# Loading x in four DMAs of 32 KiB packets, one copy per engine and tile, and the first load ahead of the barrier, in a 2x nearest-neighbour upsample

## The chip, the cores and the metric

The kernel runs on one core of one Trainium2 chip. The metric is the device time in microseconds of one execution, lower is better. Each timed version ran several times, alternating with the kernel before on the same chip. The span of a profile, from its first to its last instruction, is 1.6 us or more shorter than the device time of the same run; I compare times with times and spans with spans.

## The reference

```python
batch, channels, h, w = (16, 64, 64, 64)            # float32, scale_factor 2
for i in range(new_h):
    for j in range(new_w):
        result[:, :, i, j] = x[:, :, i // scale_factor, j // scale_factor]
```

Nothing is computed. 16.8 MB are read and 67.1 MB written; each input element goes to four places.

## The kernel before

An input row has 64 floats, 256 bytes. A tile gives each of the 128 partitions 32 input rows (8 KiB), which become 32 KiB of output. Loads take two such tiles per DMA (the first two are loaded alone). VectorE and ScalarE expand half of the rows each, with four copies per tile, one for each of the 2x2 target places. All DMAs are issued by SyncE on one queue.

```python
K = 32; rows = P * K; J = 2
...                                   # cut: checks, the sizes of the pools; group = 8, u2 has 2 buffers
for ti in range(ti0, ti0 + group):
    xt = xpool.tile([P, J, K, W], fdt, name="xt")
    if ti == 0:
        for j in range(J):
            nc.sync.dma_start(out=xt[:, j, :, :],
                in_=xf[(ti * J + j) * rows : (ti * J + j + 1) * rows, :])
    else:
        src = xf[ti * J * rows : (ti + 1) * J * rows, :]
        src = src.rearrange("(j p k) w -> p j (k w)", j=J, p=P)     # 8 KiB runs
        nc.sync.dma_start(out=xt[:, :, :, :], in_=src)
...
for t in range(ti0 * J, (ti0 + group) * J):
    ...
    u2 = upool.tile([P, K, s, W, s], fdt, name="u2")
    for ei, (lo, hi) in enumerate(((0, k_dve), (k_dve, K))):
        for hd in range(s):
            for wd in range(s):
                dst = u2[:, lo:hi, hd, :, wd]
                ...                    # cut: VectorE's tensor_copy or ScalarE's copy
    nc.sync.dma_start(out=of[r0 : r0 + rows, :], in_=u2[:, :, :, :, :])
```

Of the kernel before, what the change touches and what calls it, by code (L numbers as in the profile page):

```python
# [1 line left out]

# [4 lines left out]


@with_exitstack  # L10
def kernel(
    ctx: ExitStack,
    tc: tile.TileContext,
    x: bass.AP,
    scale_factor: bass.AP,
    out: bass.AP,
):
    nc = tc.nc
    P = nc.NUM_PARTITIONS

    s = int(scale_factor) if not isinstance(scale_factor, bass.AP) else None
    assert s is not None and s >= 1

    B, C, H, W = x.shape
    R = B * C * H
    fdt = x.dtype
    esz = 4 if fdt == mybir.dt.float32 else mybir.dt.size(fdt)

    xf = x.rearrange("b c h w -> (b c h) w")
    of = out.rearrange("b c (h hd) w -> (b c h) (hd w)", hd=s)  # L30

    K = 32
    while K > 1 and R % (P * K) != 0:
        K //= 2
    assert R % (P * K) == 0, f"{R} input rows not tileable into {P} partitions"
    rows = P * K
    ntiles = R // rows
    J = 2
    while ntiles % J != 0:
        J //= 2  # L40
    n_in = ntiles // J

    u2_bytes = K * s * W * s * esz * 2
    xt_bytes = J * K * W * esz
    group = max(1, min(n_in, (200 * 1024 - u2_bytes) // xt_bytes))
    while n_in % group != 0:
        group -= 1

    k_dve = (K + 1) // 2

    with (
        tc.tile_pool(name="xin", bufs=group) as xpool,
        tc.tile_pool(name="uexp", bufs=2) as upool,
    ):
        for ti0 in range(0, n_in, group):
            xts = {}
            for ti in range(ti0, ti0 + group):
                xt = xpool.tile([P, J, K, W], fdt, name="xt")
                if ti == 0:
                    for j in range(J):  # L60
                        nc.sync.dma_start(
                            out=xt[:, j, :, :],
                            in_=xf[(ti * J + j) * rows : (ti * J + j + 1) * rows, :],
                        )
                else:
                    src = xf[ti * J * rows : (ti + 1) * J * rows, :]
                    if J > 1:
                        src = src.rearrange("(j p k) w -> p j (k w)", j=J, p=P)
                    nc.sync.dma_start(out=xt[:, :, :, :], in_=src)
                xts[ti] = xt  # L70

            for t in range(ti0 * J, (ti0 + group) * J):
                ti, j = divmod(t, J)
                r0 = t * rows
                xt = xts[ti]

                u2 = upool.tile([P, K, s, W, s], fdt, name="u2")
                for ei, (lo, hi) in enumerate(((0, k_dve), (k_dve, K))):
                    if lo >= hi:
                        continue  # L80
                    src_ap = xt[:, j, lo:hi, :]
                    for hd in range(s):
                        for wd in range(s):
                            dst = u2[:, lo:hi, hd, :, wd]
                            if ei == 0:
                                nc.vector.tensor_copy(out=dst, in_=src_ap)  # L86
                            else:
                                nc.scalar.copy(out=dst, in_=src_ap)  # L88

                nc.sync.dma_start(out=of[r0 : r0 + rows, :], in_=u2[:, :, :, :, :])  # L90


# [1 line left out]
_INS = ['x', 'scale_factor']  # L94
_OUTS = [((16, 64, 128, 128), 'float32')]
#: Inputs that are plain numbers.
_NUMBERS = {'scale_factor': 2}


# [26 lines left out]
```

## Time and profile before

| | before |
|---|---|
| time, median (before the prediction) | 200.79 us, 200.72 to 201.0, 3 runs |
| span of the profile | 199.2 us |
| first data packet | 1.74 us |
| packets in flight without a gap | 196.2 us |
| one 8 KiB load packet | 309 to 321 ns for 97% of them, mean 317 ns (2048 of them) |
| one 32 KiB store packet | 1213 ns (2048 of them) |

The packet rows are worked out from the start, length and size of each packet in the trace. Sixteen DMA engines share the packets, so n packets of t take n x t / 16.

Lines of the page of the kernel before: span, busy time, DMA by fortieths of the span, the two queues with packets, MB and share of 16 engines, the chain that ended last, and the two groups of copies (count | busy us, mean ns | idle us before, and what ended most of it).

```profile
span 199.2 us, 246 instructions
DVE 40.0 (20%) x64; ACT 68.0 (34%) x65; POOL 0.2 (0%) x4
DMA  6999999999999999999999999999999999999995
...
q1 hardware_dynamic: 4496, 83.89, 98.5%
q14 instruction: 3, 0.02, 0.0%
...
DMA out_dram<-u 67%; ACT u L88 18%; SPq L90 3%; DMA xt<-in_x_dram 2%; ACTq L121 1%; ACTq L88 0%
...
L88 ACT COPY u<-xt 128x1024 f32<-128x1024 f32 x64 | 66.7, 1136 | 114.6 <-DMA out_dram<-u 111.0
L86 DVE COPY u<-xt 128x1024 f32<-128x1024 f32 x64 | 40.0, 690 | 141.7 <-DMA out_dram<-u 136.1
```

The queue of transfers is never idle between the first and the last slice, and both compute engines mostly wait for a store to give back an output buffer. The 18% of ScalarE in the chain of waits do not mean that ScalarE costs anything: while it expands one buffer, the other buffer's store keeps the DMA engines busy. So the time is bytes over DMA rate, plus what is lost.

The timeline of SyncE's first two microseconds (start, length, what), and pieces of the chain of waits in order of time (start, length, what):

```profile
0.73 0.86 SPq L61 DMA_DIRECT2D xt<-in_x_dram  x2
1.64 0.43 SPq L69 DMA_DIRECT2D xt<-in_x_dram  x1
```

```profile
105.30 15.10 DMA out_dram<-u
...
124.69 15.14 DMA out_dram<-u
139.92 4.21 ACT u L88 x4
144.15 15.56 DMA out_dram<-u
159.81 4.18 ACT u L88 x4
164.01 15.02 DMA out_dram<-u
```

The first load is issued at 0.73 us, after a barrier.

Four stretches of the profile before (window, its length, busy times of VectorE, ScalarE, GpSimd, clock, DMA share, GB/s): loads, loads, the turnover from loads to stores, and stores.

```profile
4.00:20.00 16.00, 4.96 (x8) 8.25 (x8) 0.00 (x0) 1.00 1.01 426
20.00:36.00 16.00, 0.00 (x0) 0.00 (x0) 0.00 (x0) 1.00 1.01 421
36.00:48.00 12.00, 0.00 (x0) 0.00 (x0) 0.00 (x0) 1.00 1.02 433
48.00:185.00 137.00, 35.02 (x56) 58.46 (x56) 0.00 (x0) 1.00 1.01 434
```

Loads run at 421 to 426 GB/s, stores at 434. GB/s of a stretch count a packet where it starts, so with 32 KiB packets a short stretch is uncertain by 2 to 4%.

### The profile page before, as it was taken

To read this page: it belongs to the slowest core of one execution; us is meant where nothing else is said; L and a number is where in the kernel's file an instruction comes from. 1 tells how busy PE (TensorE), PEld (TensorE's weight loads), DVE (VectorE), ACT (ScalarE), POOL (GpSimd) and SP (SyncE) were. 2 spreads that over 40 slices of the span, in tenths; PEclk is the share of its full clock that TensorE was granted. 3 is DMA by queue.
4 is the path that set the end of the run, shared out by engine and by line. 5 is a ranking of instruction groups with operands and counts; after the bars stand their busy time and mean duration, and the time that the engine had idled before them with its cause. 6 is when DMAs were issued, how large, how long until landed. Compare 5 with 4: busy or idle time off the path is not lost.

```text
span 199.2 us, 246 instructions
## 1 busy us (share of the span) xinstructions
DVE 40.0 (20%) x64; ACT 68.0 (34%) x65; POOL 0.2 (0%) x4
## 2 busy tenths in 40 slices
DVE  0810000000404050505050505050505050504000
ACT  2870000000444352626161708080808080808000
POOL 0000000000000000000000000000000000000000
DMA  6999999999999999999999999999999999999995
GB/s 214 423 438 421 423 421 424 421 500 421 421 421 421 421 421 441 480 447 421 421 421 421 421 421 461 474 428 428 421 421 421 424 421 467 461 421 421 428 428 217
DMA packets 4499, 83.90 MB, mean 421 GB/s; under 512 B 401, under 2 KB 401, under 8 KB 401
## 3 DMA queue, kind: packets, MB, share of 16 engines
q1 hardware_dynamic: 4496, 83.89, 98.5%
q14 instruction: 3, 0.02, 0.0%
HBM read 16.78 MB, written 67.11 MB: 421 GB/s over the span
## 4 chain that ended last, share of the span: by engine, by line
DMA 69%; ACT 18%; SPq 3%; ACTq 1%; issue 0%
DMA out_dram<-u 67%; ACT u L88 18%; SPq L90 3%; DMA xt<-in_x_dram 2%; ACTq L121 1%; ACTq L88 0%
## 5 line engine op out<-in xcount | busy, mean ns | idle before, releaser
L88 ACT COPY u<-xt 128x1024 f32<-128x1024 f32 x64 | 66.7, 1136 | 114.6 <-DMA out_dram<-u 111.0
L86 DVE COPY u<-xt 128x1024 f32<-128x1024 f32 x64 | 40.0, 690 | 141.7 <-DMA out_dram<-u 136.1
L88 ACT ACT_TABLE_LOAD x1 | 1.3, 1283 | 0.7 <-PEq L107 0.7
L107 POOL MEMSET const-uint8-127<- 128x1 uint8 x1 | 0.1, 102 | 0.0
L107 POOL MEMSET const-bfloat16-1.0<- 128x1 bf16 x1 | 0.1, 101 | 0.0
L107 POOL MEMSET const-float32-0.0<- 128x1 f32 x1 | 0.1, 99 | 0.2 <-issue 0.2
L107 POOL MEMSET const-float32-1.0<- 128x1 f32 x1 | 0.1, 98 | 0.0
## 6 DMA issues: line engine op xcount, KB each, us to landing
out_dram<-u SPq DMA_DIRECT2D x16, 4096.0 KB, 15.1
xt<-in_x_dram SPq DMA_DIRECT2D x7, 2048.0 KB, 24.4
xt<-in_x_dram SPq DMA_DIRECT2D x2, 1024.0 KB, 5.8
```

The lines of the kernel that those rows point to most:

```text
L86: nc.vector.tensor_copy(out=dst, in_=src_ap)
L88: nc.scalar.copy(out=dst, in_=src_ap)
L90: nc.sync.dma_start(out=of[r0 : r0 + rows, :], in_=u2[:, :, :, :, :])
L107: nc = _bacc.Bacc("TRN2", target_bir_lowering=False, num_devices=1)
L121: with _tile.TileContext(nc) as tc:
```

## The change

The intent: fewer and larger descriptors for the loads, fewer and larger copies, and a first load that does not wait for the barrier of the preamble. Each partition now owns 128 consecutive input rows per tile, so a load has 32 KiB runs on both sides; a store's runs of 32 KiB are then 128 KiB apart in memory. One instruction with a broadcast source (step 0) replaces four copies, and VectorE's share grows from 16 to 18 rows of 32.

```diff
+def begin_before_barrier(nc):
+    ...                    # cut: moves SyncE's first DMA into the block ahead of its first drain
+    nc.at_finalize(begin_before_barrier)
...
+    K, J = 32, 4
+    NB = R // (P * J * K)
+    xf = x.rearrange("b c h w -> (b c h) w").rearrange("(n p r) w -> n p r w", n=NB, p=P)
+    of = out.rearrange(...).rearrange("(n p r) w -> n p r w", n=NB, p=P)
+    KV = 18
...
+    for n in range(NB):
+        xt = xpool.tile([P, J * K, W], fdt, name="xt")
+        nc.sync.dma_start(out=xt[:, :, :], in_=xf[n])
...
+    def expanded(rows):
+        k = rows.shape[1]
+        return rows.unsqueeze(2).unsqueeze(4).to_broadcast([P, k, s, W, s])
...
-                for ei, (lo, hi) in enumerate(((0, k_dve), (k_dve, K))):
-                    for hd in range(s):
-                        for wd in range(s):
-                            ...
+            nc.vector.tensor_copy(out=u[:, :KV], in_=expanded(xts[n][:, r0 : r0 + KV, :]))
+            nc.scalar.copy(out=u[:, KV:], in_=expanded(xts[n][:, r0 + KV : r0 + K, :]))
+            nc.sync.dma_start(out=of[n, :, r0 : r0 + K, :], in_=u[:, :, :, :, :])
```

More of the change, by code (lines that the diff above doesn't have):

```diff
@@ L7 @@
 from concourse._compat import with_exitstack
+def begin_before_barrier(nc):
+    blocks = nc.main_func.blocks
+    main, body = blocks[0], blocks[1]
+    sp = mybir.EngineType.SP
+    load = next(i for i in body.instructions if i.engine == sp)
+    assert isinstance(load, mybir.InstDMACopy), type(load)
+    assert not (load.sync_info and load.sync_info.on_wait)
+    body.instructions = [i for i in body.instructions if i is not load]
+    kept = list(main.instructions)
+    at = next(
+        n
+        for n, i in enumerate(kept)
+        if i.engine == sp and isinstance(i, mybir.InstDrain)
+    )
+    kept.insert(at, load)
+    main.instructions = kept
 @with_exitstack
@@ L14 @@
     x: bass.AP,
-    scale_factor: bass.AP,
+    scale_factor: int,
     out: bass.AP,
@@ L18 @@
     nc = tc.nc
+    nc.at_finalize(begin_before_barrier)
     P = nc.NUM_PARTITIONS
-    s = int(scale_factor) if not isinstance(scale_factor, bass.AP) else None
-    assert s is not None and s >= 1
+    s = int(scale_factor)
     B, C, H, W = x.shape
@@ L26 @@
     fdt = x.dtype
-    esz = 4 if fdt == mybir.dt.float32 else mybir.dt.size(fdt)
-    xf = x.rearrange("b c h w -> (b c h) w")
-    of = out.rearrange("b c (h hd) w -> (b c h) (hd w)", hd=s)
-    K = 32
-    while K > 1 and R % (P * K) != 0:
-        K //= 2
-    assert R % (P * K) == 0, f"{R} input rows not tileable into {P} partitions"
-    rows = P * K
-    ntiles = R // rows
-    J = 2
-    while ntiles % J != 0:
-        J //= 2
-    n_in = ntiles // J
-    u2_bytes = K * s * W * s * esz * 2
@@ L44 @@
-    xt_bytes = J * K * W * esz
-    group = max(1, min(n_in, (200 * 1024 - u2_bytes) // xt_bytes))
-    while n_in % group != 0:
-        group -= 1
-    k_dve = (K + 1) // 2
-    with (
-        tc.tile_pool(name="xin", bufs=group) as xpool,
-        tc.tile_pool(name="uexp", bufs=2) as upool,
-    ):
-        for ti0 in range(0, n_in, group):
-            xts = {}
-            for ti in range(ti0, ti0 + group):
-                xt = xpool.tile([P, J, K, W], fdt, name="xt")
-                if ti == 0:
-                    for j in range(J):
-                        nc.sync.dma_start(
-                            out=xt[:, j, :, :],
-                            in_=xf[(ti * J + j) * rows : (ti * J + j + 1) * rows, :],
-                        )
-                else:
-                    src = xf[ti * J * rows : (ti + 1) * J * rows, :]
-                    if J > 1:
-                        src = src.rearrange("(j p k) w -> p j (k w)", j=J, p=P)
-                    nc.sync.dma_start(out=xt[:, :, :, :], in_=src)
-                xts[ti] = xt
-            for t in range(ti0 * J, (ti0 + group) * J):
-                ti, j = divmod(t, J)
-                r0 = t * rows
-                xt = xts[ti]
-                u2 = upool.tile([P, K, s, W, s], fdt, name="u2")
-                for ei, (lo, hi) in enumerate(((0, k_dve), (k_dve, K))):
-                    if lo >= hi:
-                        continue
-                    src_ap = xt[:, j, lo:hi, :]
-                    for hd in range(s):
-                        for wd in range(s):
-                            dst = u2[:, lo:hi, hd, :, wd]
-                            if ei == 0:
-                                nc.vector.tensor_copy(out=dst, in_=src_ap)
-                            else:
-                                nc.scalar.copy(out=dst, in_=src_ap)
-                nc.sync.dma_start(out=of[r0 : r0 + rows, :], in_=u2[:, :, :, :, :])
@@ new lines @@
+    K, J = 32, 4
+    NB = R // (P * J * K)
+    assert NB * P * J * K == R
+    xf = x.rearrange("b c h w -> (b c h) w").rearrange(
+        "(n p r) w -> n p r w", n=NB, p=P
+    )
+    of = out.rearrange("b c (h hd) w -> (b c h) (hd w)", hd=s).rearrange(
+        "(n p r) w -> n p r w", n=NB, p=P
+    )
+    KV = 18
+    xpool = ctx.enter_context(tc.tile_pool(name="xin", bufs=NB))
+    upool = ctx.enter_context(tc.tile_pool(name="uexp", bufs=2))
+    xts = []
+    for n in range(NB):
+        xt = xpool.tile([P, J * K, W], fdt, name="xt")
+        nc.sync.dma_start(out=xt[:, :, :], in_=xf[n])
+        xts.append(xt)
@@ new lines, in expanded @@
+    def expanded(rows):
+        k = rows.shape[1]
+        return rows.unsqueeze(2).unsqueeze(4).to_broadcast([P, k, s, W, s])
+    for n in range(NB):
+        for j in range(J):
+            r0 = j * K
+            u = upool.tile([P, K, s, W, s], fdt, name="u")
+            nc.vector.tensor_copy(
+                out=u[:, :KV], in_=expanded(xts[n][:, r0 : r0 + KV, :])
+            )
+            nc.scalar.copy(
+                out=u[:, KV:], in_=expanded(xts[n][:, r0 + KV : r0 + K, :])
+            )
+            nc.sync.dma_start(
+                out=of[n, :, r0 : r0 + K, :], in_=u[:, :, :, :, :]
+            )
```

## The prediction

> **What bounds the kernel now.** It moves 16.8 MB in and 67.1 MB out and is bound by the 16 DMA engines. The page gives 421 GB/s over a span of 199.2 us, with queue 1 busy for 98.5% of 16 engines' span. VectorE is busy 20%, ScalarE 34%. The groups of instructions put almost all their idle time down to waiting for a store to release an output buffer. The packet records in the trace give: first packet at 1.74 us, packets without a gap for 196.2 us, then about 1.2 us of landing and closing. The Trainium skill, "DMA: Bandwidth & Descriptors", section Specifications, gives a fabric ceiling of 435 GB/s; this trace's stores are next to it: a 32 KiB packet takes 1213 ns (2048 of them, very uniform), which is 432 GB/s on 16 engines. The 8 KiB load packets take 309 to 311 ns, mean 317, which is 423 GB/s or less.
>
> **What the change does.**
> 1. Loads become 512 packets of 32 KiB in place of 2048 of 8 KiB. Four 8 KiB packets cost 1240 ns, one of 32 KiB should cost 1213. Per engine: 128 x 311 = 39.8 us becomes 32 x 1213 = 38.8 us. About 1.0 us saved, a little more if the slower 8 KiB packets (340 ns) also go: 1.0 to 1.5 us.
> 2. The first load is issued in front of the barrier. The timeline shows its issue at 0.73 us, after SyncE waited 0.7 us for the barrier. It should be issued near 0.1 us, and the first packet come near 1.1 us: 0.5 to 0.65 us saved, since DMA is the whole chain.
> 3. The first tile is now 4 MB and not 1 MB: compute starts at about 11 us, not 5.6, and the first store is issued at about 16, not 9.8. Off the chain: stores queue behind the loads until about 40 us in both.
> 4. Four copies per engine and tile become one with a broadcast source. Before, ScalarE's four take 4.2 us, and the chain of waits shows that time between a store's landing and the next issue. A store takes 9.7 us of queue and two buffers alternate, so I estimate that expansion may take about 7 us before the queue runs dry. After: VectorE has 4608 elements; at one per 0.96 GHz cycle (clock from the Trainium skill, title page, NeuronCore Architecture) that is 4.8 us as an estimate, if the broadcast loses the present 690 ns per 1024. ScalarE's 3584 elements: 3.3 to 4 us. Still hidden.
> 5. Stores keep 32 KiB packets but their rows stand 128 KiB apart and not contiguous. I expect 1213 ns still.
>
> **Sum.** 199.2 - 1.1 (packets) - 0.6 (start) = 197.5 us of span; the measured time stands 1.6 us above the span, so 199.1 us. The large copies earn nothing: compute is hidden.
>
> **Time:** 199.1 us, range 198.3 to 200.3. Faster by over 2%: 0.03. Within 2%: 0.94. Slower by over 2%: 0.03.
>
> **What would show it.** Load packets at 1213 ns and about 432 GB/s in the first 40 us; first load issue near 0.1 us, first packet 0.6 us earlier; store packets unchanged at 1213 ns; expansion under 5.5 us per tile.
>
> **What would make it wrong.** A broadcast copy at two cycles an element (about 9.6 us) would starve the queue. A power-of-two pitch of 128 KiB could slow stores. The measured time may not start with SyncE's first instruction, or the early DMA may start no earlier because descriptor work is the limit; then only 1.1 us remain.

## More of the kernel before

All runs used here were at a granted clock of 1.0.

Stores land 15.0 to 15.1 us after their issue, but the one of 144.15 us needed 15.56.

## The result

| | before | after |
|---|---|---|
| time, median | 200.89 us, 200.72 to 201.04, 4 runs | 199.97 us, 199.93 to 200.07, 4 runs |
| span of the profile | 199.2 us | 198.2 us |
| first data packet | 1.74 us | 1.01 us |
| last packet ends | 197.97 us | 196.82 us |
| load packet | mean 317 ns per 8 KiB | 1213 ns per 32 KiB, but 1.2 to 2.1 us for the last two of each engine |

The ratio after to before is 0.9958 (95% interval 0.9944 to 0.9972). A ratio is the mean time of one kernel's fast runs over that of the other's of the same rounds, so it is not quite the ratio of the medians quoted here. The time lies inside the range that I gave, but the gain is 0.92 us by the medians where I had forecast 1.7.

The page after, the same lines (there is no instruction queue any more):

```profile
span 198.2 us, 145 instructions
DVE 40.9 (21%) x16; ACT 52.0 (26%) x17; POOL 0.2 (0%) x4
DMA  8999999999999999999999999999999999999994
...
q1 hardware_dynamic: 2880, 83.89, 98.8%
...
DMA out_dram<-u 70%; ACT u L81 14%; DMA xt<-in_x_dram 6%; ACTq L81 0%
...
L81 ACT COPY u<-xt 128x3584 f32<-128x3584 f32 x16 | 50.8, 3179 | 128.3 <-DMA out_dram<-u 118.0
L78 DVE COPY u<-xt 128x4608 f32<-128x4608 f32 x16 | 40.9, 2560 | 139.6 <-DMA out_dram<-u 127.3
```

SyncE's first issues, and pieces of the chain of waits:

```profile
0.00 2.15 SPq L67 DMA_DIRECT2D xt<-in_x_dram  x4
```

```profile
123.04 16.05 DMA out_dram<-u
139.18 3.19 ACT u L81
142.39 16.07 DMA out_dram<-u
158.56 3.19 ACT u L81
161.76 16.06 DMA out_dram<-u
```

The first load is issued at 0.00 us. Every store of this chain from 65 us on now takes the same 16.04 to 16.07 us to land; none is delayed as the one of 144.15 us was before. (16 in place of 15 us only because a faster expansion lets it queue longer behind its predecessor.) The same four stretches after:

```profile
4.00:20.00 16.00, 5.03 (x2) 6.26 (x2) 0.00 (x0) 1.00 1.01 436
20.00:36.00 16.00, 0.00 (x0) 0.00 (x0) 0.00 (x0) 1.00 1.02 440
36.00:48.00 12.00, 0.00 (x0) 0.00 (x0) 0.00 (x0) 1.00 1.02 404
48.00:185.00 137.00, 35.84 (x14) 44.51 (x14) 0.00 (x0) 1.00 1.00 432
```

Here is the surprise. The loads are faster, as predicted, but the stretch in which the queue turns from loads to stores fell from 433 to 404 GB/s. The DMA share is 1.02 in both: the engines are not idle there, their packets are slow. A busy row would never have shown it. Read engine by engine, the packets of one (start in ns + length in ns, the last load packets and the first stores; from the trace's packets, chained by their ends) are:

```
after:  ... 36767+1213 37976+1946 39906+1801 | 41713+1213 42922+1213 ...
before: ... 41306+321 41621+309 41925+321 | 42246+1220 43460+1213 ...
```

After, the last load packet of all 16 engines is stretched so, and of most the one before it (1.65 to 2.07 us for the last one). Before, none of the last two 8 KiB packets of an engine takes over 422 ns.

To add the pieces up I use a shortfall: the time T less (bytes moved by T) / 432.2 GB/s, with packets cut in proportion at T; 432.2 GB/s is 32768 B / 1213 ns x 16. Its growth over a stretch is the time lost there.

| span lost, us | before | after | after - before | I predicted |
|---|---|---|---|---|
| 0 to 4 us: start | 2.62 | 1.93 | -0.69 | -0.6 |
| 4 to 36 us: loads | 0.63 | -0.07 | -0.70 | -1.1 with the next row |
| 36 to 48 us: turnover | 0.15 | 0.95 | +0.80 | (none) |
| 48 to 185 us: stores | -0.22 | -0.33 | -0.11 | 0 |
| from there to the end of the span | | | -0.28 | 0 |
| sum | | | -0.98 | -1.7 |

The last row is 198.21 - 199.19 less the rows above it. So two things want explaining: the turnover, +0.80, and the 0.39 us that the stores and the end gained.

### The profile page after: what moved, and what is told of

It is laid out like the page before. It is cut to its first block, busy times and chain, and to the rows that moved or that the text cites. A ratio compares the mean times of both kernels' runs of the same rounds, so it can differ in the third digit from the quotient of the medians.

```text
span 198.2 us, 145 instructions
## 1 busy us (share of the span) xinstructions
DVE 40.9 (21%) x16; ACT 52.0 (26%) x17; POOL 0.2 (0%) x4
## 4 chain that ended last, share of the span: by engine, by line
DMA 77%; ACT 14%; issue 0%; ACTq 0%
DMA out_dram<-u 70%; ACT u L81 14%; DMA xt<-in_x_dram 6%; ACTq L81 0%
## 5 line engine op out<-in xcount | busy, mean ns | idle before, releaser
L81 ACT COPY u<-xt 128x3584 f32<-128x3584 f32 x16 | 50.8, 3179 | 128.3 <-DMA out_dram<-u 118.0
L78 DVE COPY u<-xt 128x4608 f32<-128x4608 f32 x16 | 40.9, 2560 | 139.6 <-DMA out_dram<-u 127.3
```

Source lines behind the costliest of these rows:

```text
L78: nc.vector.tensor_copy(out=u[:, :KV], in_=expanded(xts[n][:, r0 : r0 + KV, :]))
L81: nc.scalar.copy(out=u[:, KV:], in_=expanded(xts[n][:, r0 + KV : r0 + K, :]))
```

## The experiments

"Excess" below is the sum, over the packets that start within 8 us around the first turnover from loads to stores (12 us in the doubled loads), of their lengths less the usual length of their size (1213, 611 or 309 ns), over 16. It is 0.12 us before and 0.97 us after. Each version was profiled once and timed in 5 rounds (3 for h4_d2d); times are medians. All ran beside the kernel before, at 200.76 to 200.89 us in these five batches, so a comparison of two versions from different batches is good to about 0.1 us. The seven versions with the loads of the changed kernel (after, e1_barrier, e4_flat, f1_copies, f3_store8k, g1_late, g4_warm) have excesses from 0.82 to 1.12: two single profiles have to differ by more than that to mean something. Except for e2_early, which starts from the kernel before, every edit starts from the changed kernel.

### e1_barrier: the first load behind the barrier again

```diff
-    nc.at_finalize(begin_before_barrier)
```

> The changed kernel with its first load behind the barrier again. All theories: the first packet comes 0.73 us later than in the changed kernel (1.74 us, not 1.01) and everything after it moves by as much: span 198.9 us, time 200.7 us. If the early start was given back elsewhere (the turnover from loads to stores grew because the loads started earlier), the span stays at 198.2.

Measured: first packet at 1.76 us, span 199.0, time 200.71 us against 200.83 before in the same batch, ratio 1.0001 (0.9989 to 1.0013). The turnover's excess is 0.99, as in the changed kernel. So the early load is worth 0.74 us, and everything else in the change together is worth nothing that can be measured (the interval allows some 0.2 us either way).

### e2_early: the kernel before, with only the early load

```diff
+    nc.at_finalize(begin_before_barrier)        # the function is copied in as well
```

> The kernel before with only its first load in front of the barrier. If the early start is worth what the trace shows: first packet near 1.0 us, span 199.19 - 0.73 = 198.5 us, time 200.2 us. If the DMA queue merely waits later, no change, 200.9 us.

Measured: first packet at 1.00 us, time 200.14 us, 0.69 below the kernel before; ratio 0.9965 (0.9953 to 0.9976). Confirmed from the other side.

### e3_load8k: small load packets in the changed kernel

```diff
-        nc.sync.dma_start(out=xt[:, :, :], in_=xf[n])
+        for j in range(J):
+            r = slice(j * K, (j + 1) * K)
+            nc.sync.dma_start(out=xt[:, r, :], in_=xf[n][:, r, :])
```

> The changed kernel, but each 4 MB tile loaded by four DMAs of 8 KiB packets; stores untouched. Theory P (the stall of 0.97 us a DMA engine at the turnover comes from the large load packets): the last load packets are no longer slow, the turnover costs under 0.2 us, but the load phase is 0.8 us longer, so span about 198.1 and time about 199.9 us, no gain overall. Rival L (the stall comes from the stores' layout, rows 128 KiB apart): the stall stays, about 0.9 us, and the load phase is longer besides: span 199.0, time 200.8 us.

Measured: 199.51 us, ratio to before 0.9934 (0.9923 to 0.9946): faster than the change, 199.97, and the fastest correct version of all. The excess is 0.12. The same stretch of the turnover in its profile:

```profile
36.00:48.00 12.00, 0.00 (x0) 0.00 (x0) 0.00 (x0) 1.00 1.04 442
```

442 GB/s, not 404. With all 39 us of loads in 8 KiB packets the stall is gone. The version is 0.46 us faster than the change, and 0.4 us faster than theory P gave, but hardly through loads and turnover: by the shortfalls its loads from 4 to 36 us cost 0.70 us more than in the changed kernel and its turnover 0.79 less, 0.09 us in all. The rest lies in the start (shortfall at 4 us 1.70 and not 1.93) and in the growth from 185 us to the end of the span (1.46 and not 1.63). The cheaper start goes with a first tile in small packets: the five versions of the changed kernel that have it (e3_load8k, g3_first8k, h1_last32k, h3_turns8k, k2_twice8k) stand at 1.66 to 1.80 at 4 us, the twelve with 16 or 32 KiB first and the same early issue at 1.82 to 1.98. But e2_early, with small packets in the arrangement of the kernel before, has 1.95, so small packets alone do not bring it. Why is open, and so is the end.

### e4_flat: stores to contiguous memory (a wrong result, on purpose)

```diff
     of = out.rearrange("b c (h hd) w -> (b c h) (hd w)", hd=s).rearrange(
-        "(n p r) w -> n p r w", n=NB, p=P
+        "(t p r) w -> t p r w", t=NB * J, p=P
...
-                out=of[n, :, r0 : r0 + K, :], in_=u[:, :, :, :, :]
+                out=of[n * J + j], in_=u[:, :, :, :, :]
```

> The changed kernel with its stores to contiguous 4 MB blocks as the kernel before has them (rows land in the wrong place on purpose, result wrong). Theory P: the stall at the turnover stays, span 198.2, time 200.0 us. Rival L: the stall goes, load packets 30 and 31 of each engine take 1213 ns again, span 197.3, time 199.1 us.

Measured: 200.08 us, excess 0.90. The layout of the stores is not the cause; rival L falls. Nor does the 128 KiB distance slow the stores: 1213 ns a packet with and without it.

### f1_copies: four copies again

```diff
-            nc.vector.tensor_copy(out=u[:, :KV], in_=expanded(xts[n][:, r0 : r0 + KV, :]))
-            nc.scalar.copy(out=u[:, KV:], in_=expanded(xts[n][:, r0 + KV : r0 + K, :]))
+            for hd in range(s):
+                for wd in range(s):
+                    nc.vector.tensor_copy(out=u[:, :KV, hd, :, wd], in_=xts[n][:, r0 : r0 + KV, :])
+                    nc.scalar.copy(out=u[:, KV:, hd, :, wd], in_=xts[n][:, r0 + KV : r0 + K, :])
```

> The changed kernel with the one broadcast copy per engine and tile put back to four copies each (same 18/14 split). Theory I (in the kernel before, two 8 KiB instruction fetches at 154.8 us fall between the stores and hold up a few DMA engines, which then end about 0.5 us after the others; fewer instructions removed them): the fetches come back, two of them after 100 us, some engines end 0.4 us or more late, span 198.6 to 198.7, time 200.4 to 200.5 us. Rival: the fetches are harmless or don't come back, and the number of copies earns nothing, as I predicted: 200.0 us.

Measured: 200.24 us, 0.27 above the changed kernel (ratios to before 0.9974 and 0.9958; their intervals, 0.9961 to 0.9986 and 0.9944 to 0.9972, overlap, but the fastest run here, 200.18, is slower than the slowest of the changed kernel, 200.07). The fetches are back. The DMA queues from 150 to 160 us, in the kernel before, the changed kernel and this one (queue: packets, MB, share):

```profile
q1 hardware_dynamic: 146, 4.26, 99.2%
q14 instruction: 2, 0.02, 0.4%
```

```profile
q1 hardware_dynamic: 146, 4.26, 98.7%
```

```profile
q1 hardware_dynamic: 144, 4.19, 97.4%
q14 instruction: 2, 0.02, 0.4%
```

Before, the two 8 KiB packets come at 154.79 and 154.87 us, inside the store that took 15.56 us to land. At that time two store packets take 1571 and 1645 ns, and at the end of the kernel three engines finish 0.33 to 0.71 us after the thirteenth. In f1_copies the packets come at 152.86 and 154.13 us and one engine ends 0.30 us after the others. In the changed kernel there are none, and the last four engines end within 0.12 us. The link is in the packets: a store packet is stretched exactly behind each fetch (in f1_copies 1326 ns from 153.16 us and 1564 ns from 154.44 us, both on the one engine that ends last), and in the kernel before and in e2_early, which has the fetches too, the two engines with the stretched packets are the last two to end. No other store packet of f1_copies after 95 us takes over 1240 ns, so it is not the copies themselves that slow the stores. So fewer instructions did pay, though compute is hidden: a fetch holds up one or two of the 16 engines, and the slowest of them ends the kernel. Theory I holds, but the effect is smaller than it expected (0.4 to 0.5 us). The 0.27 us are not all the fetches' for certain: this profile's turnover also has an excess of 1.12, 0.15 more than the changed kernel's, and its start is 0.11 us better.

The Trainium skill, "Runtime: NRT & Kernel Launch", section Instruction fetch mechanics, says that instructions are refilled in 16 KiB blocks through a DMA queue and that crossing a block is "mostly hidden". The trace fits the size (two packets of 8 KiB among the stores; that they are one block is not shown). In this kernel, bound by DMA, the cost was not hidden: 113 to 432 ns on each store packet behind a fetch.

### f2_last8k: only the last tile in small packets

```diff
-        nc.sync.dma_start(out=xt[:, :, :], in_=xf[n])
+        if n < NB - 1:
+            nc.sync.dma_start(out=xt[:, :, :], in_=xf[n])
+        else:
+            for j in range(J):
+                r = slice(j * K, (j + 1) * K)
+                nc.sync.dma_start(out=xt[:, r, :], in_=xf[n][:, r, :])
```

> The changed kernel with only its last 4 MB tile loaded in 8 KiB packets. Theory P (only load packets in flight at the turnover matter, and large ones stall it): the turnover costs under 0.2 us and not 0.95, tile 3 costs 0.2 us more, so time 199.97 - 0.65 = 199.3 us, span 197.5. Rival (all the loads' packets have to be small, or the early rate is what counts): 199.8 to 200.1 us.

Measured: 199.82 us, excess 0.75. Theory P falls: the 32 packets of each engine ahead of the turnover are now as small as in e3_load8k, and yet the stall is there. Many of its last 8 KiB packets take 500 to 750 ns and not 309. The stretch of its turnover:

```profile
36.00:48.00 12.00, 0.00 (x0) 0.00 (x0) 0.00 (x0) 1.00 1.06 427
```

What went by before those packets matters, not only what is in flight.

### f3_store8k: the first two stores in small packets

```diff
+            parts = 4 if n == 0 and j < 2 else 1
+            q = K // parts
+            for i in range(parts):
+                nc.sync.dma_start(out=of[n, :, r0 + i * q : r0 + (i + 1) * q, :],
+                                  in_=u[:, i * q : (i + 1) * q, :, :, :])
```

> The changed kernel with its first two stores sent as four DMAs of 8 KiB packets each; loads large as in the change. Theory P1 (large load packets alone make the stall): it stays, and 16 packets' worth a DMA engine of 8 KiB cost 0.4 us more: time 200.4 us. Theory P2 (it takes a large load packet and a large store packet behind it): the stall goes, time 199.97 - 0.85 + 0.4 = 199.5 us.

Measured: 200.19 us, 0.2 under what P1 gave, excess 1.09. The stall stays (P1); the size of the store packets behind it does not make it.

### f4_turns: three turnovers

```diff
+    load(0)
+    load(1)                              # in place of all four loads
...
     for n in range(NB):
+        if n in (1, 2):
+            load(n + 1)                  # behind the four stores of the tile before
```

> The changed kernel with loads 2 and 3 each issued behind four more stores, so that the queue turns from loads to stores three times and not once. Theory P (each turnover from large loads to stores costs about 0.95 us a DMA engine): two more, time 199.97 + 1.9 = 201.9 us, and 16 slow load packets or more at each of the three. Rival (a single event at about 39 us, whatever the queue does): time stays within 0.3 us of 199.97. Turns from stores to loads may cost as well; their packets will show it.

Measured: 200.53 us, not 201.9. The first turnover, at 20 us, has an excess of 1.04 us; the second and third have 0.0 and 0.2. So it is not a fixed price for each turnover; nor is it a thing of 39 us, as the rival had it. The first turnover pays, at 20 us as at 39. The later two differ in more than their place in the row, though: each has one tile of loads ahead of it (10 us), the first has two.

### g1_late, g2_16k, g3_first8k, g4_warm

g1_late takes the tiles in another order, so that the first stores are queued late:

```diff
-    for n in range(NB):
+    for n in (2, 0, 1, 3):
```

> The changed kernel working through its tiles in the order 2, 0, 1, 3, so that the first two stores are issued near 35 and 38 us, shortly before the turnover, and not at 15.6 and 18.6. So far the stall came wherever the first stores were queued early (23 to 5 us ahead). Theory Q (what matters is how the first stores sit in the queue: early behind few waiting packets): the stall changes or goes, time down to 199.1 us. Rival (only what the loads' packets were counts): stall 0.95 us as before, time 200.0 us.

Measured: 199.99 us, excess 1.07. How long the stores had been queued does not matter; theory Q falls.

g2_16k loads half tiles:

```diff
-        nc.sync.dma_start(out=xt[:, :, :], in_=xf[n])
+        for j in range(0, J, 2):
+            r = slice(j * K, (j + 2) * K)
+            nc.sync.dma_start(out=xt[:, r, :], in_=xf[n][:, r, :])
```

> The changed kernel with eight loads of 2 MB in 16 KiB packets. If packet size sets the stall smoothly: about half, 0.4 us, with half of the rate's gain lost: time 199.7 us. If any load packet above 8 KiB, or an unhindered issue of loads, makes it: 0.9 us, time 200.1 us.

Measured: 199.59 us, excess 0.60. The stall grows with packet size, smoothly.

g3_first8k is f2_last8k the other way round (`if n > 0` large, tile 0 small):

> The changed kernel with only its first tile loaded in 8 KiB packets. The start is 0.2 us cheaper as in the version with all loads small, the first tile's rate 0.2 us dearer. If large packets later are enough for the stall: it stays at 0.95 and the time is 200.0 us. If the stall belongs to how the queue was first filled: it goes, 199.1 us.

Measured: 199.88 us, excess 0.92. Small packets at the very start do not prevent it.

g4_warm stores 128 KB of zeros early, to rows that are written again at the end:

```diff
+    early = wpool.tile([P, s, s * W], fdt, name="early")
+    nc.vector.memset(early[:, :, :], 0.0)
+    nc.scalar.dma_start(out=of[NB - 1, :, J * K - 1 : J * K, :], in_=early[:, :, :])
```

> The changed kernel with a 128 KB store of zeros to rows that are written again later, issued at the start from ScalarE's queue. Theory C (the stall is paid by the first store of all, whenever it comes, since in the version with three turnovers only the first turnover cost 1.0 us and the later ones 0 to 0.2): the stall at 38 us goes, time 199.2 us plus 0.3 for the extra bytes. Rival: the turnover still costs 0.95 us, time 200.0 to 200.4 us.

Measured: 200.43 us, excess 0.82. The early store is not what pays, so theory C falls in the form tested. It was a small one: 128 packets of 1 KiB, between 5 and 14 us, from another queue. A large early store was not tried.

### h1_last32k and h2_two8k: which tiles are small

Same edit as f2_last8k, with small packets for tiles 0 to 2 (h1_last32k) or for tiles 2 and 3 (h2_two8k).

> The changed kernel with tiles 0 to 2 in 8 KiB packets and only the last tile in 32 KiB packets. Theory H (the stall is built up by the history of the loads: some lead of the reads over the writes that grows while large packets run and shrinks slowly with small ones; one large tile ahead of a turnover gave 0 to 0.2 us in the run with three turnovers): excess of the last load packets 0.1 to 0.4 us, time 199.3 to 199.6 us. Local rival (large packets at the turnover are what counts): excess 0.95 us, time 200.2 us.

Measured: 199.76 us, excess 0.40.

> The changed kernel with tiles 0 and 1 in 32 KiB packets and tiles 2 and 3 in 8 KiB packets. Theory H: the lead left after two small tiles is less than after one (0.76 us): 0.4 to 0.6 us of excess, time 199.7 us. Rival (any large load packet, however long ago, makes the whole stall): 0.8 us or more, 199.9 us.

Measured: 199.71 us, excess 0.35.

The excess of h1_last32k is at the top of what a history expects and that of h2_two8k just under it (0.4 to 0.6); the first refutes the local rival, the second the rival that any large packet makes the whole stall. The time of h1_last32k is 0.16 us above what I had given, though.

### h3_turns8k: three turnovers with small packets

f4_turns and e3_load8k together.

> Three turnovers as in the run that had them, with all loads in 8 KiB packets. All theories: no turnover costs over 0.2 us, the first least different from the others; time 199.5 to 199.9 us. If the first turnover costs 0.9 us here as well, the packet size is not the cause, the interleaved order is.

Measured: 200.29 us; the first turnover, at 20 us, has an excess of 1.04, as with large packets, and the later ones under 0.1. This contradicts what I had expected of all theories, and the sentence that I had put down for this case blames the interleaved order. I do not follow it as it stands: g1_late to h2_two8k show that the packets' history counts. What h3_turns8k shows is that 20 us of small packets are not enough to be rid of the stall. Whether the interleaved order adds to it was not tested apart: there is no run with 20 us of loads and no further ones behind the stores. Its stretch of the first turnover, and that of f4_turns:

```profile
16.00:28.00 12.00, 0.00 (x0) 0.00 (x0) 0.00 (x0) 1.00 1.03 401
```

```profile
16.00:28.00 12.00, 1.33 (x1) 2.56 (x1) 0.00 (x0) 1.00 1.00 393
```

### h4_d2d: a copy from memory to memory between loads and stores

```diff
+    nc.sync.dma_start(
+        out=of[NB - 1, :, (J - 1) * K :, :].rearrange("p r w -> p (r w)"),
+        in_=xf[0].rearrange("p r w -> p (r w)"),
+    )
```

> The changed kernel with a 4 MB copy from x to rows of out that are written again later, HBM to HBM in 32 KiB packets, queued between the last load and the first store. It is 9.7 us or more longer; only its packets count. Theory S (the stall is the stores' first data being read from SBUF while the last loads are still being written to it): the last load packets take 1213 ns as others, excess under 0.2 us, and none at the turn from the copy to the stores. Rival (turning from reading to writing HBM, or any turn after large loads): excess 0.9 us at the end of the loads as in the changed kernel.

Measured: 210.65 us. All the last load packets take 1213 ns: that the queue goes on to write HBM does not slow them by itself. But the copy's own packets take 1.3 to 1.6 us, single ones of its last up to 2.1; the shortfall grows by 1.5 us over the copy and its turn to the stores. So theory S got its first point and not its second, and a copy that is slow for its own reasons can hide the price. That the stores' reading of SBUF is needed is supported by this, not shown.

### k1_twice32k and k2_twice8k: a load phase of double length

```diff
+    for n in range(NB):                                   # k1_twice32k; k2_twice8k the same in
+        nc.sync.dma_start(out=xts[n][:, :, :], in_=xf[n]) # 8 KiB packets, and its first loads too
```

> The changed kernel with all four tiles loaded a second time before the first store (same data, result right), 32 KiB packets. Theory H (a lead of about 1 us, kept by large packets, paid once at the turnover): 38.7 us more of loads, turnover excess 0.95 to 1.0 us as before, time 238.7 us. Rival (the turnover takes back all that the loads gained): excess about 1.9 us, time 239.6 us.

Measured: 238.16 us, excess 0.65, lower than the 0.95 that I expected.

> The same with all loads in 8 KiB packets. Theory H: no lead left at the turnover, excess under 0.15 us, and the second half of the loads runs at its own rate, 39.7 us or more: time 199.5 + 39.7 = 239.2 us or more, 0.5 us or more above the version with large packets. Rival: 0.3 to 0.5 us below the version with large packets, as with single loads.

Measured: 239.35 us, excess 0.11. The stretches from 74 to 86 us, first k1_twice32k, then k2_twice8k:

```profile
74.00:86.00 12.00, 0.00 (x0) 0.00 (x0) 0.00 (x0) 1.00 0.98 401
```

```profile
74.00:86.00 12.00, 0.00 (x0) 0.00 (x0) 0.00 (x0) 1.00 1.05 445
```

The sign turns round: with 78 us of loads the large packets win by 1.19 us, with 39 us they lost 0.46. (By the shortfalls of loads and turnover alone: 1.13 won and 0.09 lost.) The turnover did not take back twice as much; it took less. In these runs its excess was never above 1.12 us, however long the loads had gained.

### The turnover in one table

| version | load packets ahead of the first turnover | excess, us | time, us |
|---|---|---|---|
| after | 32 KiB for 39 us | 0.97 | 199.97 |
| g3_first8k | 8 KiB for 10 us, then 32 KiB | 0.92 | 199.88 |
| f2_last8k | 32 KiB, then 8 KiB for 10 us | 0.75 | 199.82 |
| g2_16k | 16 KiB for 39 us | 0.60 | 199.59 |
| h1_last32k | 8 KiB for 29 us, then 32 KiB for 10 us | 0.40 | 199.76 |
| h2_two8k | 32 KiB, then 8 KiB for 20 us | 0.35 | 199.71 |
| e3_load8k | 8 KiB for 39 us | 0.12 | 199.51 |
| f4_turns | 32 KiB for 19 us | 1.04 | 200.53 |
| h3_turns8k | 8 KiB for 19 us | 1.04 | 200.29 |
| k1_twice32k | 32 KiB for 78 us | 0.65 | 238.16 |
| k2_twice8k | 8 KiB for 80 us | 0.11 | 239.35 |

One account fits most rows: there is a debt of about 1 us from early on, due at the first turnover. While small packets run, it is worked off by roughly 0.03 us in each microsecond, after the first 15 us or so (1.0 less 0.03 x 20 leaves 0.4 for h2_two8k and 0.35 was measured; 0.03 x 10 leaves 0.7 for f2_last8k against 0.75; 0.03 x 14 leaves 0.6 for h1_last32k against 0.40 and 0.03 x 24 leaves 0.3 for e3_load8k against 0.12, so the account is good to 0.2 us and no better). Large packets keep the debt whole. The account was made after these runs; it has no term for the 16 KiB of g2_16k, and k1_twice32k, 0.65 in place of 1.0, does not fit it.

The rate is about the amount by which small packets are slower. In e3_load8k the 8 KiB packets take 309 ns on the mean from 5 to 14 us and 314 ns from 18 to 36 us, and the shortfall then grows by 0.024 us in each microsecond. So with 40 us of loads the slow small packets of the kernel before cost about what they saved: 0.70 us of loads against 0.80 us at the turnover. That the first is the payment of the second is not shown, and k2_twice8k speaks against it: its packets stay at 314 ns from 38 to 74 us, and its shortfall grows by another 0.87 us, when after 39 us of such packets e3_load8k had only 0.12 left to pay.

What the debt is made of, no run shows. My guess is that the engines read ahead of their writes by up to some 26 KB each (an estimate: 1 us at 27 GB/s, a sixteenth of 432), and that at the turnover they read the stores' data from SBUF while that much load data is still to be written into it. The records of packets do not separate reading from writing, h4_d2d supports it in half, and the 0.65 of k1_twice32k, the lasting slowness in k2_twice8k and the nearly free second and third turnovers of f4_turns are not derived from it. That stays open.

## Why the prediction was wrong

- What bounds the kernel: right. DMA stays at nine tenths in all but the first and last of the fortieths, and stores keep 1213 ns a packet at a distance of 128 KiB too (e4_flat).
- Step 2, the early load, 0.5 to 0.65 us: right and a little small. The first packet came 0.73 us earlier; e1_barrier and e2_early give 0.74 and 0.69 us of time. This is most of the result.
- **Step 1 failed: "About 1.0 us saved, a little more if the slower 8 KiB packets (340 ns) also go: 1.0 to 1.5 us", in the sum "- 1.1 (packets)".** Its observable, load packets of 1213 ns at about 432 GB/s in the first 40 us, came true until 38 us, and the loads did gain 0.70 us in the shortfall from 4 to 36 us. But the sum took a packet's usual length times the number of packets for the length of the phase. The end of the phase is not usual: the last load packet of every engine is stretched, and of most the one before it, and the turnover costs 0.95 us where it had cost 0.15. In the place of -1.1 stands -0.70 + 0.80 = +0.10. e3_load8k shows that both terms go with the packet size (its loads 0.70 us dearer, its turnover 0.79 cheaper), k1_twice32k and k2_twice8k that the gain in rate is real but lost again at this length of loads. Why the turnover charges it stays open.
- Step 3, the later start of compute: about right, and harmless. Compute began at 12.35 us and the first store was issued at 15.55, with loads in the queue until 42.
- Step 4, expansion stays hidden: right. But "The large copies earn nothing: compute is hidden" was wrong. With four copies the changed kernel is 0.27 us slower (f1_copies), and two instruction fetches are back among the stores. The before page had the queue "instruction" with 3 packets, and the chain of waits one store of 15.56 us among stores of 15.1; both were there to be read.
- Also in step 4, VectorE was expected at 4.8 us if the broadcast lost its rate. It takes 2560 ns for 4608 elements, 0.56 ns an element against 690 / 1024 = 0.67 before: the broadcast source kept the rate.
- Of the sum, -0.6 was -0.69, -1.1 was +0.10, 0 was -0.39 (stores and end). The two errors partly cancel; that the time still fell into the range is luck.

## What to carry to other kernels

When a phase is bound by DMA, do not cost it as packets times their usual time alone: look at the packets at its ends, where the queue turns from loads to stores, and measure GB/s there, since the busy share stays full while packets are stretched. Larger packets in a load phase of about 40 us bought nothing clear of noise here and paid only when the phase was twice as long; try the smaller size beside it. Read every DMA queue on the page, the instruction queue too: fewer instructions can matter in a kernel whose compute engines are idle, because the fetches share the DMA engines, and the slowest engine ends the kernel.

## What the Trainium skill lacked or had wrong

- "Runtime: NRT & Kernel Launch", section Instruction fetch mechanics, calls the cost of crossing a block of instructions "mostly hidden". Here each of the two fetch packets of 8 KiB among the stores stretched a store packet by 113 to 432 ns, the engines concerned ended last, and the version with them was 0.27 us slower (f1_copies against the changed kernel).
- "DMA: Bandwidth & Descriptors" has no price for the turn of one queue from loads to stores. The runs show 0.1 to 1.1 us a DMA engine at the first turnover, depending on the size of the load packets and on how long they ran, and 0 to 0.2 us at later ones.
- The same page, section Measured, gives GB/s by the size of a DMA and no rate by the size of a packet above the small ones. The runs: 309 ns for 8 KiB, 611 ns for 16 KiB and 1213 ns for 32 KiB in each of 16 engines, 424, 429 and 432 GB/s; after some 15 us of loads the 8 KiB packets took 314 ns on the mean.
